# Three output stores moved to one place in the DMA queue of a batched matrix multiply

## The chip, the cores and the metric

The kernel runs on one core of a Trainium2 chip. The metric is the device time of one execution in microseconds (us), the median of several. All the runs told of here are in the fast state, so they may be compared with one another.

## The reference

```python
batch, dim_i, dim_j, dim_k = 32, 256, 512, 384      # all float32
def reference(x, y):                                 # x: b i j, y: b j k
    return np.einsum('bij,bjk->bik', x, y)
```

Thirty-two independent products of 256x512 by 512x384. x has 16.8 MB, y 25.2 MB, the result 12.6 MB.

## The kernel before

The kernel takes the batch in eight groups of four. For each group, x is loaded (2 MB), cast and transposed on VectorE (step T), y is loaded (3 MB) and cast, also on VectorE (R), TensorE multiplies (M), ScalarE copies most of the PSUM banks to an output tile (C) and VectorE the rest (D), and the tile is stored (S, 1.5 MB). A list of steps fixes the order in which each engine gets its instructions. All 24 transfers are issued by SyncE (SP), in the order of the list:

```python
O_BUFS = 5
PLAN = """
x0 x1 y0
T0 x2 y1
T1 R0 M0 C0 x3 y2
T2 D0 R1 M1 C1 x4 y3 S0
T3 D1 R2 M2 C2 x5 y4 S1
T4 D2 R3 M3 C3 x6 y5
T5 D3 R4 M4 C4 x7 y6 S2
T6 D4 R5 M5 C5 y7
T7 D5 R6 M6 C6 R7 M7 C7 D7 S3 S4 S5 S6 S7
"""
# ...
x_pool = ctx.enter_context(tc.tile_pool(name="x_pool", bufs=2))
y_pool = ctx.enter_context(tc.tile_pool(name="y_pool", bufs=2))
o_pool = ctx.enter_context(tc.tile_pool(name="o_pool", bufs=O_BUFS))
# ...
for step in PLAN.split():
    parts[step[0]](int(step[1:]))        # load_x, load_y, transpose_x, round_y, multiply, ...
```

So a load of group n waits in SP until group n-2 has been cast out of its buffer (x3's cast ended at 41.02 us, x5 was issued at 41.05), and the output tile of group 5 uses the buffer that S0 empties.

Of the kernel before, what the change touches and what calls it, by code (L numbers as in the profile page):

```python
# [1 line left out]

# [4 lines left out]


MM_DT = mybir.dt.float16
F32 = mybir.dt.float32  # L10
P = 128


Q = 4
STEP = 4
O_BUFS = 5
WIDE_GROUPS = 6




PLAN = """
x0 x1 y0
T0 x2 y1
T1 R0 M0 C0 x3 y2
T2 D0 R1 M1 C1 x4 y3 S0
T3 D1 R2 M2 C2 x5 y4 S1
T4 D2 R3 M3 C3 x6 y5
T5 D3 R4 M4 C4 x7 y6 S2
T6 D4 R5 M5 C5 y7  # L30
T7 D5 R6 M6 C6 R7 M7 C7 D7 S3 S4 S5 S6 S7
"""


@with_exitstack
def kernel(
    ctx: ExitStack,
    tc: tile.TileContext,
    x: bass.AP,
    y: bass.AP,  # L40
    out: bass.AP,
):
    nc = tc.nc

    B, I, J = x.shape
    _, _, K = y.shape

    PQ = P // Q
    R = I // PQ
    T = J // PQ  # L50
    TW = T // 2
    NE = I // P
    N = B // Q

    x_pool = ctx.enter_context(tc.tile_pool(name="x_pool", bufs=2))
    y_pool = ctx.enter_context(tc.tile_pool(name="y_pool", bufs=2))
    xr_pool = ctx.enter_context(tc.tile_pool(name="xr_pool", bufs=1))
    xt_pool = ctx.enter_context(tc.tile_pool(name="xt_pool", bufs=3))
    yr_pool = ctx.enter_context(tc.tile_pool(name="yr_pool", bufs=2))
    o_pool = ctx.enter_context(tc.tile_pool(name="o_pool", bufs=O_BUFS))  # L60
    psum_pool = ctx.enter_context(
        tc.tile_pool(name="psum", bufs=1, space=bass.MemoryType.PSUM)
    )

    keep = tc.keep_in_program_order

    bank = {
        (e, g): psum_pool.tile([P, K], F32, name=f"o_ps_{e}_{g}") for e in range(NE) for g in range(Q)
    }




    x_of, y_of, xt_of, yr_of, ps_of, o_of = {}, {}, {}, {}, {}, {}

    def width(n):
        return PQ if n < WIDE_GROUPS else 2 * PQ

    def on_vector(n, e, g):
        if n < WIDE_GROUPS:  # L80
            return (e, g) == (NE - 1, Q - 1)
        return n == N - 1 and g % 2 == 1

    def load_x(n):
        x_of[n] = x_pool.tile([P, R, J], F32, name="x_sb")
        keep(
            nc.sync.dma_start(  # L87
                out=x_of[n],
                in_=x[n * Q : (n + 1) * Q].rearrange("g (p r) j -> (g p) r j", r=R),
            )  # L90
        )

    def load_y(n):
        y_of[n] = y_pool.tile([P, T, K], F32, name="y_sb")
        keep(
            nc.sync.dma_start(
                out=y_of[n],
                in_=y[n * Q : (n + 1) * Q].rearrange("g (q t) k -> (g q) t k", t=T),
            )
        )  # L100

    def transpose_x(n):


        x_r = xr_pool.tile([P, R, J], MM_DT, name="x_r")
        keep(nc.vector.tensor_copy(x_r, x_of.pop(n)))  # L106
        xt_of[n] = xt_pool.tile([P, NE, TW, P], F32, name="xt_sb")
        b = width(n) // PQ
        src = x_r.bitcast(F32).rearrange("p (b h e) (q t) -> p b e t h q", b=b, e=NE, t=TW)
        dst = xt_of[n].rearrange("p e t (h s b) -> p b e t h s", s=PQ, b=b)  # L110
        for e in range(NE):
            for c in range(b):
                keep(nc.vector.transpose(dst[:, c, e], src[:, c, e]))  # L113

    def round_y(n):
        y_sb = y_of.pop(n)
        yr_of[n] = yr_pool.tile([P, T, K], MM_DT, name="y_r")
        for a in range(0, T, STEP):
            keep(nc.vector.tensor_copy(yr_of[n][:, a : a + STEP], y_sb[:, a : a + STEP]))  # L119

    def multiply(n):
        xt = xt_of.pop(n).bitcast(MM_DT).rearrange("p e t (m c) -> p e t m c", c=2)
        y_r = yr_of.pop(n)
        o_of[n] = o_pool.tile([P, R, K], F32, name="o_sb")
        for e in range(NE):
            for g in range(Q):
                ps_of[n, e, g] = bank[e, g]
            for t in range(T):
                for g in range(Q):
                    s = slice(g * PQ, (g + 1) * PQ)  # L130
                    keep(
                        nc.tensor.matmul(  # L132
                            ps_of[n, e, g],
                            xt[s, e, t // 2, :, t % 2],
                            y_r[s, t],
                            start=(t == 0),
                            stop=(t == T - 1),
                        )
                    )

    def collect(n, vector):
        w = width(n)
        per = P // w
        copy = nc.vector.tensor_copy if vector else nc.scalar.copy
        o = o_of[n].rearrange("p (u f) k -> p u f k", u=Q // per)
        for e in range(NE):
            for g in range(Q):
                if on_vector(n, e, g) != vector:
                    continue
                ps = ps_of.pop((n, e, g))  # L150
                a = g % per * w
                for h in range(per):
                    keep(copy(o[a : a + w, g // per, h * NE + e], ps[h * w : (h + 1) * w]))  # L153

    def store(n):
        w = width(n)
        per = P // w
        dst = out[n * Q : (n + 1) * Q].rearrange("(u g) (s f) k -> (g s) u f k", g=per, s=w)
        keep(
            nc.sync.dma_start(  # L160
                out=dst, in_=o_of.pop(n).rearrange("p (u f) k -> p u f k", u=Q // per)
            )
        )

    parts = {
        "x": load_x,
        "y": load_y,
        "T": transpose_x,
        "R": round_y,
        "M": multiply,  # L170
        "C": lambda n: collect(n, False),
        "D": lambda n: collect(n, True),
        "S": store,
    }
    for step in PLAN.split():
        parts[step[0]](int(step[1:]))


# [1 line left out]
_INS = ['x', 'y']  # L180
_OUTS = [((32, 256, 384), 'float32')]


# [23 lines left out]
```

## Time and profile before

| what | value | how to read it |
|---|---|---|
| time | 134.82 us | median of 3 runs, 134.75 to 134.98 |
| DMA | full in 38 of 40 slices | the row of tenths; 9 is 90% or more |
| VectorE, ScalarE, TensorE busy | 72%, 69%, 47% | shares of the span of 133.2 us |
| last landing of a store | 132.4 us | issue of S7 plus its time to landing |

The lines of the page, of SP's timeline and of the DMA view are shown in the prediction. In a timeline line the columns are start in us, duration in us, engine and source line, operation, tile written and read, count. In the DMA view, the last number of a line is the time from issue to landing.

### The profile page before, as it was taken

The numbers are of one execution on the slowest core, as the hardware profiler recorded it, in microseconds if no ns is written. First come the engines' busy times: TensorE is split into PE (matmuls) and PEld (weight loads), VectorE is DVE, ScalarE is ACT, GpSimd is POOL, SyncE is SP. The second block draws the span as 40 slices with busy tenths as digits, with TensorE's granted clock in tenths as the row PEclk, the third lists the DMA queues.
The fourth block names the chain that finished last, engine by engine and source line by source line (L and its number), as shares of the span: only waits on it lengthen the run. The fifth ranks groups of instructions, "written<-read, shape, count | busy, mean of one in ns | idle before, by whom it ended". The sixth has DMA issues, their size and how long they took to land.

```text
span 133.2 us, 2437 instructions
## 1 busy us (share of the span) xinstructions
PE 62.5 (47%) x1024; PEld 33.6 (25%) x1024; DVE 96.1 (72%) x92; ACT 91.7 (69%) x193; POOL 0.2 (0%) x4
## 2 busy tenths in 40 slices
PE   0000004980499049915981079400993198788000
PEld 0000002550245025502540035200451054445000
DVE  0049999699979998999059990899999950764500
ACT  3000000089999999999999997999739999997400
POOL 0000000000000000000000000000000000000000
PEclk9999999999559955996589658975579756999855
DMA  5999999999999999999999999999999999999992
GB/s 118 408 448 448 421 411 448 435 450 389 453 428 428 408 450 443 362 403 440 443 462 389 426 430 445 448 394 445 421 443 403 443 450 398 417 429 413 411 415 103
DMA packets 3723, 54.68 MB, mean 410 GB/s; under 512 B 384, under 2 KB 384, under 8 KB 896
## 3 DMA queue, kind: packets, MB, share of 16 engines
q1 hardware_dynamic: 3712, 54.53, 96.8%
q8 instruction: 8, 0.13, 0.4%
q14 instruction: 3, 0.02, 0.0%
HBM read 41.94 MB, written 12.58 MB: 409 GB/s over the span
## 4 chain that ended last, share of the span: by engine, by line
DMA 39%; ACT 22%; DVE 17%; PE 12%; issue 4%; DVEq 1%; SPq 0%
DMA x_sb<-in_x_dram 39%; ACT o_sb L153 22%; PE o_ps L132 12%; DVE xt_sb L113 6%; DVE x_r L106 5%; DVE o_sb L153 4%; DVE y_r L119 1%; DVEq L202 1%; SPq L160 0%; DVEq L106 0%; SPq L87 0%
## 5 line engine op out<-in xcount | busy, mean ns | idle before, releaser
L153 ACT COPY o_sb<-o_ps 32x384 f32<-32x384 f32 (+1 forms) x192 | 90.4, 471 | 32.4 <-PE o_ps L132 26.6
L132 PE MATMUL o_ps<-y_r,xt_sb 32*128 32x384 f16 x1024 | 62.5, 403 | 60.5 <-DVE y_r L119 51.9
L132 PEld LDWEIGHTS <-xt_sb 32*128 32x128 f16 x1024 | 33.6, 114 | 89.0 <-DVE y_r L119 37.7
L119 DVE CAST y_r<-y_sb 128x1536 f16<-128x1536 f32 x32 | 28.5, 953 | 6.1 <-DMA y_sb<-in_y_dram 5.9
L106 DVE CAST x_r<-x_sb 128x4096 f16<-128x4096 f32 x8 | 18.3, 2293 | 19.3 <-DMA x_sb<-in_x_dram 19.3
L113 DVE STREAM_TRANSPOSE xt_sb<-x_r 128x1024 f32<-128x1024 f32 (+1 forms) x20 | 31.6, 1626 | 0.3
L153 DVE COPY o_sb<-o_ps 32x384 f32<-32x384 f32 (+1 forms) x32 | 17.8, 556 | 3.5 <-PE o_ps L132 1.7
L153 ACT ACT_TABLE_LOAD x1 | 1.3, 1283 | 0.7 <-PEq L191 0.7
L191 POOL MEMSET const-bfloat16-1.0<- 128x1 bf16 x1 | 0.1, 102 | 0.0
L191 POOL MEMSET const-uint8-127<- 128x1 uint8 x1 | 0.1, 102 | 0.0
L191 POOL MEMSET const-float32-0.0<- 128x1 f32 x1 | 0.1, 99 | 0.2 <-issue 0.2
L191 POOL MEMSET const-float32-1.0<- 128x1 f32 x1 | 0.1, 99 | 0.0
## 6 DMA issues: line engine op xcount, KB each, us to landing
y_sb<-in_y_dram SPq DMA_DIRECT2D x8, 3072.0 KB, 22.3
x_sb<-in_x_dram SPq DMA_DIRECT2D x8, 2048.0 KB, 22.4
out_dram<-o_sb SPq DMA_DIRECT2D x8, 1536.0 KB, 21.9
```

What stands on the lines that cost most here:

```text
L106: keep(nc.vector.tensor_copy(x_r, x_of.pop(n)))
L113: keep(nc.vector.transpose(dst[:, c, e], src[:, c, e]))
L119: keep(nc.vector.tensor_copy(yr_of[n][:, a : a + STEP], y_sb[:, a : a + STEP]))
L132: nc.tensor.matmul(ps_of[n, e, g], xt[s, e, t // 2, :, t % 2], y_r[s, t], start=(t == 0), stop=(t == T - 1),)
L153: keep(copy(o[a : a + w, g // per, h * NE + e], ps[h * w : (h + 1) * w]))
L191: nc = _bacc.Bacc("TRN2", target_bir_lowering=False, num_devices=1)
L202: with _tile.TileContext(nc) as tc:
```

## The change

It gathers S0, S1 and S2, which stood singly between loads, behind the eighth load of x and ahead of the seventh of y. The intent can be read from the place: the loads that feed the engines go first, and the stores wait until nothing urgent is left. The whole diff:

```diff
-T2 D0 R1 M1 C1 x4 y3 S0
-T3 D1 R2 M2 C2 x5 y4 S1
+T2 D0 R1 M1 C1 x4 y3
+T3 D1 R2 M2 C2 x5 y4
 T4 D2 R3 M3 C3 x6 y5
-T5 D3 R4 M4 C4 x7 y6 S2
+T5 D3 R4 M4 C4 x7 S0 S1 S2 y6
```

## The prediction

> **What bounds the kernel now.** I read the page's forty slices first, for which engine is never idle.
>
> ```profile
> span 133.2 us, 2437 instructions
> PE 62.5 (47%) x1024; PEld 33.6 (25%) x1024; DVE 96.1 (72%) x92; ACT 91.7 (69%) x193; POOL 0.2 (0%) x4
> ...
> DMA  5999999999999999999999999999999999999992
> GB/s 118 408 448 448 421 411 448 435 450 389 453 428 428 408 450 443 362 403 440 443 462 389 426 430 445 448 394 445 421 443 403 443 450 398 417 429 413 411 415 103
> ...
> HBM read 41.94 MB, written 12.58 MB: 409 GB/s over the span
> ```
>
> No compute engine is over 72%, but the DMA row is full from the second slice to the last but one. 54.5 MB at some 425 GB/s, about what the inner slices average, take about 128 us, which with start and end is the span. So the transfers bound it, and there is one queue for all of them, fed by SP in program order. Next I took SP's own timeline, which gives every issue:
>
> ```profile
> 40.58 0.35 SPq L160 DMA_DIRECT2D out_dram<-o_sb  x1
> 41.05 0.36 SPq L87 DMA_DIRECT2D x_sb<-in_x_dram  x1
> 50.91 0.33 SPq L96 DMA_DIRECT2D y_sb<-in_y_dram  x1
> 54.16 0.34 SPq L160 DMA_DIRECT2D out_dram<-o_sb  x1
> 54.60 0.43 SPq L87 DMA_DIRECT2D x_sb<-in_x_dram  x1
> 63.49 0.33 SPq L96 DMA_DIRECT2D y_sb<-in_y_dram  x1
> 70.34 0.33 SPq L87 DMA_DIRECT2D x_sb<-in_x_dram  x1
> 80.18 0.33 SPq L96 DMA_DIRECT2D y_sb<-in_y_dram  x1
> 80.60 0.38 SPq L160 DMA_DIRECT2D out_dram<-o_sb  x1
> 96.10 0.33 SPq L96 DMA_DIRECT2D y_sb<-in_y_dram  x1
> 96.48 29.15 SPq L160 DMA_DIRECT2D out_dram<-o_sb  x5
> ```
>
> These are S0, x5, y4, S1, x6, y5, x7, y6, S2, y7 and S3 to S7. Asked of a window around one issue, the DMA view gives that transfer's time to landing. For the windows at 80.5, 96.4 and 125.2 us:
>
> ```profile
> y_sb<-in_y_dram SPq DMA_DIRECT2D x1, 3072.0 KB, 23.0
> out_dram<-o_sb SPq DMA_DIRECT2D x1, 1536.0 KB, 26.3
> ...
> y_sb<-in_y_dram SPq DMA_DIRECT2D x1, 3072.0 KB, 18.0
> out_dram<-o_sb SPq DMA_DIRECT2D x1, 1536.0 KB, 21.3
> ...
> out_dram<-o_sb SPq DMA_DIRECT2D x1, 1536.0 KB, 7.1
> ```
>
> So y6 lands at 80.18 + 23.0 = 103.2, S2 at 106.9, y7 at 114.1, S3 at 117.8, S7 at 132.4. Done for all 24, the landings come in exactly the order of issue, one behind the other, and the step from one to the next depends on the size alone: 4.85 to 4.89 us for an x of 2 MB (one of 4.74), 3.64 to 3.71 for a store, 7.2 to 7.3 for a y of 3 MB (y4 to y7). y1, y2 and y3 took about 8.2, 7.8 and 8.1; the packet records show PE's instruction fetches, 1 us each, at 30.8, 44.3 and 58.3 us among them. I take x 4.88, y 7.27, S 3.67. A store between loads costs the same 3.7 as a store among stores (S0 3.71, S4 3.64).
>
> The chain of waits names "DMA x_sb<-in_x_dram 39%" and ACT 22%, and ends in copies. I don't take that as the bound: it walks through compute that runs beside a full queue.
>
> [...] So a store that isn't ready holds up every load behind it in SP, and the order of the list is the order of the bytes; this is how SP's timeline looks (x5 at 41.05, 0.47 us behind S0's issue). [...] Here the first load is issued from 0.73 to 1.17 and its first packet starts at 1.79: 0.6 us, or 1.05 from the start of the issue. [...]
>
> **The change, part by part.** No instruction of PE, DVE, ACT or POOL changes, and the same 24 transfers are issued. S0 moves from ahead of x5 to behind x7, S1 from ahead of x6 to behind x7, S2 from behind y6 to ahead of it. Nothing removed or added in bytes: three stores are 11.0 us of queue in either order. The sum is zero unless the queue runs dry somewhere, or the last stores are late. Both I worked out by hand from the durations above: DVE cast of x 2.29, transposes 3.9, D 2.27, R 3.56, ACT 13.58 per group (112 copies in 54.32), second half of a group's matmuls 2.78.
>
> Up to 50.9 us nothing differs but S0's place: x5 was held by its own buffer until 41.05, not by S0. y3 lands at 59.34 in both. From there, each landing is the one before plus the step; the issue is from the buffer it needs:
>
> x5 lands 64.2 (was 67.9), issued 41.05.
> y4 71.5 (75.2), issued 50.9.
> x6 76.4 (83.7), issued 53.6, at the end of x4's cast; before it stood behind S1 until 54.6.
> y5 83.6 (91.0), issued 63.5, after R3.
> x7 88.5 (95.9): x5's cast runs 64.3 to 66.6, so issued 66.6 (70.3).
> S0, S1, S2 92.2, 95.9, 99.5: issued 67.0, 67.4, 67.8, as C2 ends at 26.99 + 3 x 13.58 = 67.7. SP blocks on none for over a microsecond.
> y6 106.8 (103.2): needs R4. T5 to 70.5, D3 after M3's second half (67.8 + 2.8) to 72.9, R4 to 76.5; issued 76.5.
> y7 114.1 (114.1): needs R5. T6 76.5 to 82.8, D4 after C3 (81.3) and 2.8 of PE, to 86.4, R5 to 90.0; issued 90.0 (96.1).
> S3 117.7, S4 121.4, S5 125.1, S6 128.8, S7 132.4 (132.4).
>
> Each transfer is issued at least 12 us ahead of its turn, except S6 and S7, so the queue doesn't run dry before those. By y7 the same bytes have passed in both orders, so y7 and all behind it land when they did.
>
> The tail is what needs care, since y6 comes 3.6 us later. Before, R6 began at 104.70, held by D5 rather than by y6's landing at 103.2, so the real delay is 106.85 - 104.70 = 2.15 us; R6 then ends at 110.4. On the other side ACT is earlier: C4 81.3 to 94.9, C5 94.9 to 108.4 (before 98.7 to 112.28), since y5 no longer keeps M5 waiting. C5 writes the fifth output buffer again, which S0 frees at 92.2, 2.7 us before. C6 then waits for M6's first half instead of for C5. PE began it at 106.49 before and took 5.30 for 63 matmuls; now it can begin after R6's first quarter at 107.8 and ends between 111.3 (the fast pace of 2.78, held by R6's last quarter) and 113.2. So C6 begins between 111.3 and 113.2 against 112.28, and S7, 12.98 us behind in the trace (125.26 - 112.28), is issued between 124.3 and 126.2. Its data starts 1.05 later, at the latest 127.3; S6 occupies the queue until about 128.4. S7 is still not waited for.
>
> **Rivals.** (1) The later y6 goes through to the end: 3.6 us more, 138.4. For it: y6 is the only load that comes later, and R6, M6, C6, M7, C7 and S7 follow it. Against: 1.5 us of it lay behind D5 already, ACT gains 3.8 us ahead of it, and S7 has some 2 us to spare (issue at 125.26 against a need near 127.2). Even the bad end of the tail gives 0 to 1 us.
> (2) The loads come up to 7.4 us earlier, compute's waits vanish (ACT idle 0.86 us before C4 and 2.98 before C5), and the end moves up by those 3.8: 131.0. For it: the chain runs through these copies. Against: S3 to S7 are 18.4 us of queue behind y7, and y7's landing doesn't move.
> (3) The queue runs dry because stores block loads behind them or because S0 and C5's buffer form a ring of waits: a dry spell of n us costs n. Against: C2 is over when x7 is issued, and some 20 us of loads are queued then. Seven transfers would be in flight, against five before; if the queue took fewer, SP would stand until y4 lands at 71.5, still ahead of y6's issue at 76.5.
> (4) Reads and writes overlap worse when three stores stand together. The steps of S3 to S7 (3.64 to 3.70) speak against: 0.1 us at most.
>
> **Range and chances.** My sum is zero, so 134.8, the time before. Runs of before lie within 0.23 us. The instruction fetches can fall on other DMA engines or other transfers, up to a step of 0.9 us for one, and the tail may cost up to 1: I take 134.3 to 135.5. For faster over 2% (under 132.1) bytes would have to vanish or the queue to speed up: 0.01. Slower over 2% (above 137.5) needs rival 1 or 3 almost in full: 0.03.
>
> **What would show it.** The DMA row full in every slice but first and last; landings of x7 near 88.5, y6 near 106.8, y7 near 114.1, S7 near 132.4; R6 starting right at y6's landing, DVE's idle before it ended by a DMA of y; ACT without its 3 us gap before C5 but with one of about 3 us before C6. I am wrong if y7 lands later than 115, if a slice falls visibly under 9 in the DMA row, or if S7 is issued after 127.2.

## The result, and the profile after

The changed kernel took 134.38 us (6 runs, 134.34 to 134.66), the kernel before in the same rounds 134.83 us (6 runs, 134.75 to 135.07). Ratios in this document are the mean time of one kernel's fast runs over that of the other's of the same rounds, so not quite the ratio of the medians: here 0.9969, with a 95% interval of 0.9956 to 0.9982. The time is the same at 2%, and inside the range; the 0.3% is small and yet clear of the noise, and the prediction had zero for it.

The page of the changed kernel, its span, busy times and DMA rows:

```profile
span 132.9 us, 2437 instructions
...
PE 61.5 (46%) x1024; PEld 34.9 (26%) x1024; DVE 96.1 (72%) x92; ACT 91.7 (69%) x193; POOL 0.2 (0%) x4
...
DMA  4999999999999999999999999999999999999993
GB/s 109 429 424 441 451 414 429 446 429 412 419 471 407 404 437 441 432 409 446 429 417 414 456 432 402 414 419 429 429 464 429 414 451 400 419 425 412 400 412 141
```

The row is as full as before, 90% or more in 38 of 40 slices, so the queue didn't run dry. SP's timeline after:

```profile
41.63 0.33 SPq L87 DMA_DIRECT2D x_sb<-in_x_dram  x1
51.49 0.33 SPq L96 DMA_DIRECT2D y_sb<-in_y_dram  x1
53.83 0.33 SPq L87 DMA_DIRECT2D x_sb<-in_x_dram  x1
63.72 0.33 SPq L96 DMA_DIRECT2D y_sb<-in_y_dram  x1
66.03 0.33 SPq L87 DMA_DIRECT2D x_sb<-in_x_dram  x1
66.41 1.80 SPq L160 DMA_DIRECT2D out_dram<-o_sb  x3
76.62 13.93 SPq L96 DMA_DIRECT2D y_sb<-in_y_dram  x2
90.64 35.31 SPq L160 DMA_DIRECT2D out_dram<-o_sb  x5
```

The three stores leave within 1.8 us behind x7. S0 and S1 don't make SP wait; S2 (issued at 67.88) does for some 0.6 us, until the copies of its group end at 67.8. Seven of SP's transfers are then in flight (y4, x6, y5, x7 and the three stores; y4 lands first, at 70.92), and no wait of SP for the queue shows. The DMA view in narrow windows at 76.6, 90.2 and 125.6 us (y6, y7, S7):

```profile
y_sb<-in_y_dram SPq DMA_DIRECT2D x1, 3072.0 KB, 29.6
...
y_sb<-in_y_dram SPq DMA_DIRECT2D x1, 3072.0 KB, 23.5
...
out_dram<-o_sb SPq DMA_DIRECT2D x1, 1536.0 KB, 6.5
```

So y6 lands at 76.62 + 29.57 = 106.2, y7 at 113.7 and S7 at 132.06. The landings of all 24, from the trace's records (a "step" is a landing less the landing ahead of it; S7's landing is the sum of all steps):

| transfer | predicted | after | before |
|---|---|---|---|
| y3 | 59.3 | 58.73 | 59.34 |
| x7 | 88.5 | 87.98 | 95.89 |
| S2 | 99.5 | 98.93 | 106.88 |
| y6 | 106.8 | 106.19 | 103.19 |
| y7 | 114.1 | 113.69 | 114.11 |
| S7 | 132.4 | 132.06 | 132.40 |

From y3 on, all of them are 0.3 to 0.6 us ahead of the prediction. What is gained is there when y3 lands. The steps ahead of y3 differ in both directions (x0 0.10 and y2 0.51 us shorter, y1 0.69 and x4 0.14 longer) and lose 0.2 us together; y3's own step is 7.31 us instead of 8.13. Up to there the only difference in the queue is what stands right behind y3: x5 instead of S0.

ScalarE's timeline (ACT), first before, then after; in brackets its idle time before a stretch and what ended it:

```profile
26.99 54.32 ACT L153 COPY o_sb<-o_ps 32x384 f32<-32x384 f32 x112 [24.98 <-PE o_ps L132]
82.17 13.56 ACT L153 COPY o_sb<-o_ps 32x384 f32<-32x384 f32 x28 [0.86 <-PE o_ps L132]
98.70 23.38 ACT L153 COPY o_sb<-o_ps 32x384 f32<-32x384 f32 x48 [2.98 <-issue]
```

```profile
27.09 81.51 ACT L153 COPY o_sb<-o_ps 32x384 f32<-32x384 f32 x168 [25.08 <-PE o_ps L132]
112.60 9.80 ACT L153 COPY o_sb<-o_ps 64x384 f32<-64x384 f32 x20 [4.00 <-issue]
```

The waits before groups 4 and 5 (0.86 and 2.98 us) are gone: 168 copies, the first six groups, run without a break to 108.6. All of it is given back in one gap of 4.00 us before group 6, because y6 comes later. VectorE shows the same from its side; the cast R6 before, and after:

```profile
104.70 3.57 DVE L119 CAST y_r<-y_sb 128x1536 f16<-128x1536 f32 x4
```

```profile
106.21 3.56 DVE L119 CAST y_r<-y_sb 128x1536 f16<-128x1536 f32 x4 [5.99 <-DMA y_sb<-in_y_dram]
```

Before, R6 stood behind other work of VectorE; after, VectorE is idle for 5.99 us until y6 lands. ScalarE thus reaches group 6 at 112.60 instead of about 112.28, and S7 is issued at 125.58 instead of 125.26, with no effect on its landing, which stays 3.7 us behind S6's.

### The profile page after: what moved, and what is told of

Read it like the earlier page. It is cut to its first block, busy times and chain, and to the rows that moved or that the text cites. A ratio compares the mean times of both kernels' runs of the same rounds, so it can differ in the third digit from the quotient of the medians.

```text
span 132.9 us, 2437 instructions
## 1 busy us (share of the span) xinstructions
PE 61.5 (46%) x1024; PEld 34.9 (26%) x1024; DVE 96.1 (72%) x92; ACT 91.7 (69%) x193; POOL 0.2 (0%) x4
## 4 chain that ended last, share of the span: by engine, by line
DMA 45%; DVE 19%; ACT 15%; PE 10%; issue 4%; DVEq 1%
DMA x_sb<-in_x_dram 22%; DMA y_sb<-in_y_dram 22%; ACT o_sb L153 15%; PE o_ps L132 10%; DVE xt_sb L113 6%; DVE x_r L106 5%; DVE o_sb L153 4%; DVE y_r L119 4%; DVEq L202 1%; DVEq L106 0%
## 5 line engine op out<-in xcount | busy, mean ns | idle before, releaser
L132 PE MATMUL o_ps<-y_r,xt_sb 32*128 32x384 f16 x1024 | 61.5, 399 | 61.7 <-DVE y_r L119 52.3
L132 PEld LDWEIGHTS <-xt_sb 32*128 32x128 f16 x1024 | 34.9, 113 | 87.9 <-DVE y_r L119 32.8
```

Source lines behind the costliest of these rows:

```text
L132: nc.tensor.matmul(ps_of[n, e, g], xt[s, e, t // 2, :, t % 2], y_r[s, t], start=(t == 0), stop=(t == T - 1),)
```

## The experiments

Twelve kernels, in three calls; kernels of one call share the runs of the kernel before (11 in each call). Diffs are against the changed kernel if nothing else is said. Two questions: does the working hold (queue never dry, a tail with slack, load order of no account), and where do the 0.3% come from?

| run | what it is | time, us | ratio to before | 95% interval |
|---|---|---|---|---|
| r_after | the changed kernel again | 134.39 | 0.9970 | 0.9946 to 0.9994 |
| s2_alone | S2 moved, S0 and S1 as before | 134.79 | 0.9994 | 0.9972 to 1.0017 |
| s01_alone | S0 and S1 moved, S2 as before | 134.55 | 0.9977 | 0.9954 to 1.0001 |
| one_matmul | changed, one of 16 matmul steps | 133.76 | 0.9921 | 0.9896 to 0.9946 |
| dry | S0 S1 S2 together ahead of x5 | 143.09 | 1.0611 | 1.0586 to 1.0636 |
| s3_early | changed, S3 ahead of y6 too | 136.90 | 1.0173 | 1.0123 to 1.0223 |
| y6_first | changed, y6 ahead of the stores | 134.40 | 0.9967 | 0.9944 to 0.9991 |
| narrow | changed, 15 of 16 matmuls narrow | 134.52 | 0.9970 | 0.9952 to 0.9989 |
| s0_back | changed, S0 back behind y3 | 134.73 | 0.9981 | 0.9963 to 0.9998 |
| s0_after_x5 | before, S0 behind x5 | 134.85 | 0.9994 | 0.9982 to 1.0006 |
| s0_ahead_y3 | before, S0 ahead of y3 | 135.08 | 1.0012 | 0.9998 to 1.0026 |
| before_one_matmul | before, one of 16 matmul steps | 134.63 | 0.9980 | 0.9955 to 1.0005 |

### The change once more

> The changed kernel unaltered, for the 0.3% by which it came out ahead. If the order of the stores causes the gain, it comes again: 134.4, ratio to before 0.995 to 0.998. If it was the luck of where PE's instruction fetches fell in those runs, the ratio is anywhere from 0.994 to 1.003, and in the trace the last landing moves with the sum of the extra steps of the loads (before 2.3 us in y1 to y3, after 1.55 in y1 and 0.2 in y7).

The gain came again, 0.9970, in another call. In the trace y1's step was 8.32, y3's 7.31, and S7 landed at 131.68.

### Each part alone

S2 moved alone, against the kernel before:

```diff
-T5 D3 R4 M4 C4 x7 y6 S2
+T5 D3 R4 M4 C4 x7 S2 y6
```

> One part alone: S2 ahead of y6, S0 and S1 left singly where they stood before. Four separate runs of stores in the queue, as before. My sum (nothing, the queue stays full and y7 has the same bytes ahead of it): within 0.4 us of before. The rival that each break between loads and stores costs some 0.2 us: exactly before, 134.8. The rival that a later y6 goes through to the end: 1 to 3 us more, since compute is as late here as before while y6 lands near 106.9.

Nothing: 0.9994. y6 landed at 106.99, later by 3.8 us than before; the C5 of this kernel began at 98.79, as late as before, and S7 left at 125.76. VectorE stood idle for y6 here as well:

```profile
107.01 3.56 DVE L119 CAST y_r<-y_sb 128x1536 f16<-128x1536 f32 x4 [2.19 <-DMA y_sb<-in_y_dram]
```

So the later y6 doesn't go through to the end, not even without the head start that ScalarE has in the changed kernel. y3's step was 8.26.

S0 and S1 moved, S2 left behind y6:

```diff
-T5 D3 R4 M4 C4 x7 S0 S1 S2 y6
+T5 D3 R4 M4 C4 x7 S0 S1 y6 S2
```

> The other part alone: S0 and S1 together behind x7, S2 behind y6 as before. Three runs of stores in the queue. My sum: within 0.4 us of before. Rival of 0.2 us per break: 134.6, half way. y6 should land near 103.2 again and R6 begin there, with y7 near 114 and S7 near 132.2.

0.9977, between the rival's half way and the full gain; the interval holds both, and just holds no gain at all. The trace says more: y3's step 7.32, S7 landing at 131.63, as early as in the changed kernel's own second trace. y6 landed at 102.36 and R6 began at 102.39, so compute ran further ahead (S7 was issued at 123.78), and the end did not move for it.

### An earlier seventh y, and a later one

```diff
-T5 D3 R4 M4 C4 x7 S0 S1 S2 y6
+T5 D3 R4 M4 C4 x7 y6 S0 S1 S2
```

> The three stores one place later, between y6 and y7. y6 lands near 95.5 instead of 106.2; S0 lands near 99, so C5 waits for its output buffer some 4 us longer (from 95 to 99), and C6 follows C5 at about 113. y7 has the same bytes ahead and lands near 113.7, S7 is issued near 126. My sum: 134.4, within 0.4. The rival that earlier loads shorten the end: 2 us or more less. The rival that the buffer wait passes on: 4 us more.

134.40, as the changed kernel. y6 landed at 94.98 instead of 106.19, S0 at 98.64. ScalarE's timeline shows the buffer wait that was expected:

```profile
98.74 23.38 ACT L153 COPY o_sb<-o_ps 32x384 f32<-32x384 f32 x48 [3.90 <-DMA out_dram<-o_sb]
```

Group 5's copies stood 3.90 us for S0's landing. S7 left at 125.30 and landed at 131.51. A load that comes 11 us earlier and a wait of ScalarE of 4 us are both hidden by the queue ahead of S7.

With a fourth store ahead of y6:

```diff
-T5 D3 R4 M4 C4 x7 S0 S1 S2 y6
+T5 D3 R4 M4 C4 x7 S0 S1 S2 S3 y6
-T7 D5 R6 M6 C6 R7 M7 C7 D7 S3 S4 S5 S6 S7
+T7 D5 R6 M6 C6 R7 M7 C7 D7 S4 S5 S6 S7
```

> A fourth store, S3, in the same place: y6 and y7 land another 3.7 us later (near 109.9 and 117.4). The tail bound then shows if I read its slack right: R6 from 109.9, M6's first half 5.4 us from the first quarter at 110.9, C6 from 116.3, S7 issued 12.98 later at 129.3, data from 130.4, landing near 134.5: 2.4 us over the changed kernel, 136.8. If the tail has more slack than I think, 134.4; if a later load passes on whole, 138.1.

136.90, ratio 1.0173, which the verdict at 2% leaves unclear. The four runs lie in two pairs (136.08 and 136.19, 137.61 and 137.82), so that the median falls where no run is, and its closeness to 136.8 is luck. The trace is of the lower pair (136.19). y6 landed at 109.67 and y7 at 116.96. ScalarE's line for group 6:

```profile
115.19 9.80 ACT L153 COPY o_sb<-o_ps 64x384 f32<-64x384 f32 x20 [7.29 <-issue]
```

The gap before group 6 has grown from 4.00 to 7.29 us, S6 was issued at 123.06 and S7 at 128.17 (expected 129.3), and now the queue waits, but for S6 and not for S7 as I had expected. S6's step is 5.41 us where the others take 3.7; S7's is 3.53. S6 was issued 1.6 us ahead of S5's landing, and it took 7.0 us from issue to landing, where I reckon 1.05 and a step of 3.67 for a store that finds the queue empty:

```profile
out_dram<-o_sb SPq DMA_DIRECT2D x1, 1536.0 KB, 7.0
```

S7 landed at 133.59, 1.5 us after the changed kernel's. This is the limit of the change: three stores fit ahead of y6, a fourth comes out at the end.

### The stores where the queue can run dry

```diff
-T3 D1 R2 M2 C2 x5 y4
-T4 D2 R3 M3 C3 x6 y5
-T5 D3 R4 M4 C4 x7 S0 S1 S2 y6
+T3 D1 R2 M2 C2
+T4 D2 S0 S1 S2 x5 y4 R3 M3 C3 x6 y5
+T5 D3 R4 M4 C4 x7 y6
```

> The three stores together as in the change, but ahead of x5 instead of behind x7: SP must stand at S2 until C2 is over at 67.7 us, with S0 and S1 the last work in the queue. If the sum is zero only because the queue never runs dry, this costs its dry spell: y3 lands at 58.7, S1 at 66.1, S2 is issued at 67.8 and lands at 72.7 instead of 69.7, so 3.0 us later for all that follows, S7 at about 135.2, time 137.4, slower by 2.0 to 2.5%. If order is of no account as long as the bytes are equal: 134.4.

143.09, three times the loss that I expected. The page's DMA row, with its hole, then SP's and ScalarE's timelines:

```profile
DMA  5999999999999999991899999999999998995974
```

```profile
39.88 27.50 SPq L160 DMA_DIRECT2D out_dram<-o_sb  x3
```

```profile
94.03 36.97 ACT L153 COPY o_sb<-o_ps 32x384 f32<-32x384 f32 x76 [13.43 <-PE o_ps L132]
```

SP stands 27.5 us in the three stores, and seven loads stand behind it. S2 is issued at 67.05 into an empty queue and lands at 74.39: 7.3 us from issue, where I had reckoned 4.9; 29 of its 128 packets take 0.53 to 1.01 us instead of 0.46. Its step is 7.94 us, 4.3 over a store's 3.65. That is the dry spell, and it isn't all. x5 and y4 land at 79.3 and 86.6, ScalarE gets nothing for 13.43 us, and this lateness of compute comes out at the end: S6 is issued at 129.06, when S5 is about to land (130.30), and its step is 6.12, 2.5 over. y7's step is 1.1 over, with slow packets ahead of S3 of which more below. These three are 7.9 of the 8.0 us by which S7 lands later (140.06 against 132.06); the rest cancels. My expectation counted the first term alone, and that too low.

### What PE's instruction fetches cost

With one of the 16 steps of each product, a wrong result on purpose:

```diff
-            for t in range(T):
+            for t in range(1):
-                            stop=(t == T - 1),
+                            stop=(t == 0),
```

> The changed kernel with the first of the 16 steps of each matmul alone: 64 matmuls in place of 1024, a wrong result on purpose. PE's instructions are then few enough to be there from the start. If the fetches of PE's instructions on the DMA engines make the extra 1.5 to 2.3 us of y1 to y3, the records hold none of these fetches, every y takes 7.3 us, and the time is 132.4 to 133.0. If the extra has nothing to do with PE, it stays at 134.4. If it comes from PE reading SBUF beside the transfers, it falls too, but then it falls as well when the matmuls are kept and made narrower (a run of its own).

And with all the matmuls, 15 of 16 of them narrow, also wrong on purpose:

```diff
-                            ps_of[n, e, g],
+                            ps_of[n, e, g] if t == 0 else ps_of[n, e, g][:, :96],
-                            y_r[s, t],
+                            y_r[s, t] if t == 0 else y_r[s, t, :96],
```

> The changed kernel with all 1024 matmuls, but 15 of 16 of them 96 columns wide instead of 384: a wrong result on purpose, PE reads far less of SBUF and issues as many instructions. If instruction fetches make the extra time of y1 to y3: eight fetches again and 134.4, within 0.4. If PE's reading beside the transfers makes it: as with one matmul, some 1.5 us less.

The queues of the changed kernel, and of the one with one matmul, from their pages:

```profile
q1 hardware_dynamic: 3712, 54.53, 96.9%
q8 instruction: 8, 0.13, 0.4%
q14 instruction: 3, 0.02, 0.0%
```

```profile
q1 hardware_dynamic: 3712, 54.53, 97.4%
q14 instruction: 3, 0.02, 0.0%
```

The eight packets of the first instruction queue (16384 bytes and 0.89 to 1.11 us each in the changed kernel) come with PE's program: with 128 PE instructions in place of 2048 they are gone. y1's step is then 7.30 us; in every trace with the fetches it is between 7.67 and 8.85. A transfer leaves 16 landing events in the trace, and what is called its landing here is the last. Before the change there is a fetch of 1.06 us at 30.8 us, and y1's last event is at 33.74 and the one ahead of it at 32.90; with one matmul they are at 32.91 and 32.86. So one event of sixteen comes late by 0.84 us, and y1's landing with it. Narrow matmuls keep the eight fetches, y1's 7.95 and the time (134.52). So the cause of y1's extra is the fetching, not PE's reading of SBUF. But the size was wrong: 133.76 is 0.6 us under the changed kernel of the same call, not 1.4 to 2.0. The extra steps of the loads don't add up at the end; in the kernel without fetches small ones appear elsewhere (y5 0.25, S4 0.27 over). The eight fetches of the changed kernel take 8.25 us together, spread over 16 engines 0.5 us an engine (an estimate from these two numbers, if they spread evenly), and that is the size found. In this kernel, whose DMA row is full in 38 of 40 slices, the time was 0.6 us shorter without the fetches and most of the matmuls, and unchanged with the fetches and narrow matmuls.

### Where the first store stands

By now y3's step was long, 7.96 to 8.26 us, in each trace with S0 right behind y3 (before, s2_alone, dry), and at most 7.73 in each of the others. I had put y3's extra down to a fetch at 58.3 us; that fetch is there in both kinds. Three kernels move S0 alone, the first against the changed kernel, the others against the kernel before:

```diff
-T2 D0 R1 M1 C1 x4 y3
+T2 D0 R1 M1 C1 x4 y3 S0
-T5 D3 R4 M4 C4 x7 S0 S1 S2 y6
+T5 D3 R4 M4 C4 x7 S1 S2 y6
```

> What is open is the 0.3%. In the three traces where S0 stands right behind y3, y3's step is 8.0 to 8.3 us; in the others 7.3. This is the changed kernel with S0 alone put back behind y3; S1 and S2 stay behind x7. If that neighbourhood is the cause: y3 takes 8.0 again and the time is that of before, 134.8 to 135.0. If each break between loads and stores costs 0.2 us (three runs of stores here): half way, as with S0 and S1 moved and S2 left. If neither: 134.4 as with the change, y3 7.3.

```diff
-T2 D0 R1 M1 C1 x4 y3 S0
-T3 D1 R2 M2 C2 x5 y4 S1
+T2 D0 R1 M1 C1 x4 y3
+T3 D1 R2 M2 C2 x5 S0 y4 S1
```

> The kernel before with S0 one place later, behind x5 (y3 x5 S0 y4 S1); four runs of stores as before. If S0 behind y3 is the cause: y3 7.3, no slow packets elsewhere, ratio to before 0.997. If the first store, when it comes early, slows whatever load is just ahead of it: y3 7.3, but x5 5.3 to 5.9, and the time of before. If breaks cost: the time of before, with no long step.

```diff
-T2 D0 R1 M1 C1 x4 y3 S0
+T2 D0 R1 M1 C1 x4 S0 y3
```

> The kernel before with S0 one place earlier, ahead of y3 (x4 S0 y3 x5). S0 is ready at 40.6 us, so y3 is issued near 41.0 against its turn at some 55: not dry. If S0 behind y3 is the cause: y3 7.3, ratio 0.997. If the first store slows the load ahead of it: x4 over 5.3 instead of 4.75, and the time of before. If breaks cost: the time of before, no long step.

The steps in the traces (us), with the usual ones 4.88 for an x and 7.30 for a y:

| kernel | x4 | y3 | x5 | S0 stands behind | S7 lands |
|---|---|---|---|---|---|
| before | 4.74 | **8.13** | 4.88 | y3 | 132.40 |
| s0_back | 4.74 | **8.25** | 4.87 | y3 | 132.34 |
| s0_after_x5 | 4.73 | 7.30 | **5.55** | x5 | 132.24 |
| s0_ahead_y3 | **5.68** | 7.30 | 4.89 | x4 | 132.12 |
| changed | 4.88 | 7.31 | 4.90 | x7 | 132.06 |
| changed, again | 4.74 | 7.31 | 5.12 | x7 | 131.68 |

The long step goes where S0 goes: it is the load just ahead of it, in all of these kernels with S0 early. The packets show it directly. Before the change, 15 of y3's packets that start between 54.1 and 56.6 us take 1.02 to 1.68 us instead of 0.92, and S0's first packet starts at 56.41; in the changed kernel no packet of y3 that starts after 52 us takes more than 0.92. In s0_after_x5 such a burst stands at 59 to 61 us, in s0_ahead_y3 at 47 to 49, and S0's first packet starts at 61.22 and 49.08. Where the queue stays full, later stores have no such burst ahead of them (before the change y4, ahead of S1, takes 7.27 us, y6, ahead of S2, 7.30, and y7, ahead of S3, 7.23). When S0 itself stands behind x7 or y6, a few slow packets at most are left (two in the changed kernel, 0.75 and 0.89 us instead of 0.61; six in narrow), and x7's step stays at 4.87 to 4.89. The dry kernel is an exception: besides y3's burst it has one in y7, ahead of S3 (114 to 117 us, up to 2.16 us a packet, step 8.37), so it need not be the very first store. So the rival of the single neighbour y3 falls, the one of 0.2 us for each break falls (s0_back has three runs of stores and y3's long step back), and what I called the first store slowing the load ahead of it stands, as far as it goes.

In time: the correct kernels with S0 late (the changed one in two calls, s01_alone and y6_first; s3_early has a late tail and is left aside) have ratios of 0.9967 to 0.9977, the four correct ones with S0 early, the dry one left aside, 0.9981 to 1.0012. The groups don't overlap, though intervals across them do: r_after's reaches 0.9994, s01_alone's 1.0001, and s0_back's begins at 0.9963. In landings of S7 the early ones, with the kernel before, are at 132.12 to 132.56, the late ones at 131.51 to 132.06.

The 16 landing events tell how much of this the burst makes. From x4's landing to y3's, the mean over the 16 advances by 7.6 us before and 7.7 in s2_alone and s0_back, but by 7.28 to 7.35 in the four traces with S0 late. At y7, the last load, the mean is at 112.48 to 112.62 in the five with S0 early and at 112.24 to 112.34 in those with S0 late. So with S0 early the average landing is about 0.25 us late at y7, as much as the burst puts it back; that is some half of the 0.45 us. How much reaches the end depends also on which of the 16 events comes last, and they are 2.5 us apart by then (y7 before: 111.58 to 114.11). By S7 the mean says less (131.13 before and after): in the changed kernel S7's first event comes 4.5 us behind S6's first (130.59 and 126.05), before the change 4.0 (130.29 and 126.27). That the burst makes the whole of the 0.3% is therefore likely, and not shown to the tenth.

Last, the kernel before with the edit of one_matmul:

> The kernel before with one of the 16 steps of each matmul alone (wrong on purpose), so without PE's instruction fetches; the changed kernel in this form took 133.76, ratio 0.992, with all steps of y1 to y3 at 7.3. If y3's extra needs the DMA engines that the fetches have put behind the others, it is gone: y3 7.3, time 133.8, no difference between the two orders. If it is S0's own: y3 about 7.8 to 8.2, time 134.2 to 134.4, ratio to before 0.995.

Between the two: 134.63, 0.9980 (0.9955 to 1.0005). The burst is there, 15 slow packets from 54.1 to 56.1 us, so it doesn't need PE's fetches. But y3's step is only 7.54, and another long step, 4.26 us in S3, has come from somewhere. In the mean over the 16 landings y3 advances by 7.52, against 7.30 in the changed kernel with one matmul, nearly the difference that it makes with the fetches; in the last landing less of it shows. The ratio of that kernel was 0.9921 in its call, and the two intervals don't touch: without the fetches too the order is worth something.

What makes such a burst stays open, and so does why there is next to none when S0 stands behind x7. In those kernels S0 comes some 30 us later and another store stands right behind it. Neither alone rules a burst out, as the dry kernel shows: S1 stood behind S0 from 53.46, before S0's first packet at 56.24, and y3 had a burst all the same (7 packets, step 7.96); and the burst in y7 came late, with S4 issued behind S3.

No correct kernel beats the changed one by more than the noise: y6_first and s01_alone have its time.

## Why the prediction was right or wrong

**The bound and the queue.** Right. The DMA row is full in 38 of 40 slices before and after, landings come in order of issue in both traces, and most steps are the predicted ones (y1's and y3's apart). That a store that isn't ready holds up the loads behind it doesn't show in the prediction's example: x5, issued at 41.05, had waited for its own buffer. It shows in x6, whose buffer was free at 53.6 and which left at 54.60, behind S1 at 54.16, and above all in dry, where SP stood 27.50 us in the stores and x5 left at 67.43; there the condition was the point.

**The hand-worked issues.** Right to within 0.7 us: x6 at 53.8 (predicted 53.6), x7 66.0 (66.6), y6 76.6 (76.5), y7 90.2 (90.0).

**The tail.** Right in its course, too simple in its limit. R6 began at y6's landing, C6 at 112.60 (between 111.3 and 113.2; M6's first half took the slow pace), S7 left at 125.58 (124.3 to 126.2), and its last landing was not held up. The prediction looked for the limit at S7, with some 2 us to spare. In s2_alone S7 left at 125.76 without harm; in s3_early, with group 6 another 2.6 us later, the store that held the queue up was S6, since a store whose data finds the queue just emptied took 7.0 to 7.4 us from issue to landing (S6 in s3_early; S2 and S6 in dry) and not the 4.7 of the working.

**Rival 1**, the later y6 going through: refuted by s2_alone. **Rival 2**, earlier loads shortening the end: refuted by y6_first and s01_alone, where loads come 11 and 4 us earlier than in the changed kernel for nothing. **Rival 3**, a dry queue: not in the change (no wait of SP for the queue with seven transfers in flight); real in dry, and there costlier than "a dry spell of n us costs n": 4.3 us of dry spell, and 8.0 us at the end, of which 2.5 by late compute and 1.1 by slow packets in y7.

**The sum.** It was said to be zero and was -0.4 us. The measured 134.38 is 0.1 us inside the low end of the range, and that end had been set for the chance of where the fetches fall, not for the cause found: that the range held is in part luck. The step that failed is "the step from one to the next depends on the size alone", and with it "three stores are 11.0 us of queue in either order". It rested on reading the long early steps as "the packet records show PE's instruction fetches, 1 us each, at 30.8, 44.3 and 58.3 us among them". For y1 that holds. For y3 it doesn't: its extra of 0.8 us belongs to S0 right behind it and moves with it. Rival 4's "0.1 us at most" rests on the same reading: I looked at the steps of stores only, which are indeed 3.7 everywhere, and not at the load ahead of the first one.

## What to carry to other kernels

In a queue that was full from end to end, the order of what was in it moved little time by itself (0.3%); ask instead whether an issue can block the loads behind it until the queue is empty, and whether the last stores still leave before their turn (in s3_early S6 left 1.6 us ahead of S5's landing, and its step was 5.41 us instead of 3.7). A blocked queue can cost more than its own gap: in dry ScalarE got nothing for 13.43 us, compute came late at the end, and a gap of 4.3 us cost 8.0. Before putting an odd step down to something that happens at the same moment, move the suspect and see whether the step moves with it.
